# A two-block transformer kernel: the FFN's first gate projection taken one token block at a time, with half of its weights split ahead of the stage before

## The chip, the cores and the metric

The kernel runs on 1 core of one Trainium2 chip. The metric is the device time of one execution in microseconds; lower is better. Each version is run several times, and medians are compared.

## What is computed

The reference runs 256 tokens of width 2048 through a first block (two layers of several kinds of attention) and a second block of two layers. Only the second block is touched. Cut to what matters:

```python
for l in range(DEPTH):                      # DEPTH = 2
    u = rms_norm_2(h, norm_pre_mix[l])
    p = u @ w_in[l]                         # four recurrent mixers
    ...
    mixed = concatenate([o_ret, o_hgrn, o_ml, o_rw]) @ w_out[l]
    h = h + rms_norm_2(mixed, norm_post_mix[l])
    u = rms_norm_2(h, norm_pre_ffn[l])
    ffn = (silu(u @ w_ffn_gate[l]) * (u @ w_ffn_up[l])) @ w_ffn_down[l]
    h = h + rms_norm_2(ffn, norm_post_ffn[l])
```

The change sits at the two places, one in each layer, where the mixing stage ends and the FFN begins.

## The kernel before

The 256 tokens are two token blocks of 128 rows (`m` = 0, 1); the width of 2048 is 16 channel blocks of 128 (`kt`) in four groups (`g`). All products are float32 ones made of three float32r products: `weights` (line 211) loads 512 KB of a weight matrix into a tile `wraw`, ScalarE rounds it into `whi` (line 217), VectorE takes the rest into `wlo` (line 218), and `mm3` (line 223) issues hi x hi, hi x lo and lo x hi. One such load carries two channel blocks by 512 output columns; with both token blocks it feeds 12 matmuls of 512 columns. `wraw`, `whi` and `wlo` have three buffers each, so that a load waits until the split of the load three before it is done, and a split waits until TensorE is done with the weights three before. All loads are issued by SyncE's queue in a fixed order; a load that has to wait holds up all that stand behind it.

`mixing` (line 1639) ends with `out_group` (line 288) for the fourth mixer: eight loads of `w_out`, called O1 to O8 below. Then `old` (line 1675) fetches the eight tiles of the residual stream from DRAM (`keep`, 256 KB each). `last_group` (line 1585) takes the last mixer's eight loads of `w_out`, called L0 to L7 below: L0 to L3 as usual; L4 to L7 go into tiles of the tag `xt`, and these two column blocks are finished for token block 0 first, then for token block 1. VectorE adds each result to `acc` (line 1594), ScalarE squares it (line 1596), VectorE multiplies by a gain (lines 1598 and 1633). From the sums of squares a chain of small VectorE operations makes the reciprocal root (lines 1622, 1623 and 378 to 384), and `add_scaled` (line 1634) forms the new `X` from it.

`ffn` (line 1685) turns `X` on TensorE (line 317, into the two PSUM banks `t`), and `put` splits the turned tiles into `xt` on ScalarE (line 310) and VectorE (line 311). With `apart=2` the first two of the four groups are turned for token block 0 first and token block 1 after it, and the other two for both together. `by_tokens` (line 226) then goes through the 16 channel blocks, each with both token blocks, for 512 columns of the gate, then of the up projection; 11 such column blocks follow each other.

The order on each engine is made by a scheduler that moves instructions of the written program past each other, by its own estimate of when each can start; it is fixed before the run.

Of the kernel before, what the change touches and what calls it, by code (L numbers as in the profile page):

```python
# [11 lines left out]
FR = mybir.dt.float32r  # L12
# [6 lines left out]
P = 128  # L19
# [115 lines left out]
def halves(x):  # L135

    return [x[:, m] for m in range(2)]


class Emitter:  # L140
# [84 lines left out]
    def by_tokens(self, xg, w, c0, n):  # L225

        out = [self.bank("m") for _ in range(2)]
        j = min(16, 1 << int(math.log2(1024 // n)))
        for k in range(0, 16, j):
            wt = self.weights(w[k * P : (k + j) * P, c0 : c0 + n], j, n)  # L230
            for i in range(j):
                kt = k + i
                for m in range(2):
                    x = self.x_part(xg, kt, slice(m * P, m * P + P))
                    self.mm3(out[m][:, :n], x, [q[:, i] for q in wt], kt == 0, kt == 15)
            next(self.side, None)
        return [o[:, :n] for o in out]

    def by_channels(self, xg, w, c0, n):

# [1398 lines left out]
    def mixing(self, l, X):  # L1639
        nc = self.nc  # L1640
        w = self.a["w_in_2"][l]
        self.phase(**BANKS_MIX)
        keep = self.dp.tile([4, P, 2, 512], FT, name="keep")
        xg = self.x_pairs(X, self.c(f"premix{l}"))
        rows = self.row_scale_of(X)
        self.R = Later(lambda i: self.spread_rows(rows["r"]))

        def table(m):
            tb = self.t([P, 4, 64], "rtab")
            for i, (n, f) in enumerate((("cos64", 1.0), ("sin64", 1.0), ("cos64", 0.125), ("sin64", 0.125))):  # L1650
                nc.vector.tensor_scalar(tb[:, i], self.c(n)[:, m * 64 : m * 64 + 64], rows["r"][:, m : m + 1], f,
                                        OP.mult, OP.mult)
            return tb

        tabs = Later(table)
        ys = [self.pair("yt") for _ in range(4)]
        with self.using(x="r", small="esmall"):
            self.rwkv(l, X, keep, xg, w, ys[3])
        gates = self.mlstm_gates(l, xg, w, rows)
        for hf in range(2):  # L1660
            self.mlstm(l, hf, xg, w, rows, gates, ys[2])
        self.hgrn(l, 0, xg, w, ys[1])
        acc = [halves(self.t([P, 2, 512], "X")) for _ in range(4)]
        wo = self.a["w_out_2"][l]
        self.out_group(ys[2], wo, 2 * 512, acc, True)
        self.hgrn(l, 1, xg, w, ys[1])
        self.retention(0, xg, w, rows, tabs, ys[0])
        self.out_group(ys[1], wo, 512, acc, False)
        self.retention(1, xg, w, rows, tabs, ys[0])
        for _ in self.side:  # L1670
            pass
        self.out_group(ys[3], wo, 3 * 512, acc, False)

        def old(g, m):

            x = self.t([P, 512], "g2")
            nc.vector.tensor_copy(x[:, :1], acc[3][1][:, :1])
            nc.sync.dma_start(x, keep[g, :, m])
            return x

        olds = [[old(g, m) for m in range(2)] for g in range(4)]
        pg, r = self.last_group(ys[0], wo, 0, acc, self.a["norm_post_mix_2"][l])
        return self.add_scaled(acc, acc, pg, r, olds)

    def ffn(self, l, X):
        nc = self.nc
        self.phase(**BANKS_FFN)
        wg, wu, wd = (self.a[f"w_ffn_{n}_2"][l] for n in ("gate", "up", "down"))
        xg = self.x_pairs(X, self.c(f"preffn{l}"), apart=2)
        rows = self.row_scale_of(X)  # L1690
        acc = [[self.t([P, 512], "r2") for _ in range(2)] for _ in range(4)]
        last = None
        for g in range(11):
            ps = self.by_tokens(xg, wg, g * 512, 512)
            s = [self.t([P, 512], "g2") for _ in range(2)]
            for m in range(2):
                nc.scalar.activation(s[m], ps[m], AF.Silu, scale=rows["r"][:, m : m + 1])
            ps = self.by_tokens(xg, wu, g * 512, 512)
            for m in range(2):
                nc.vector.scalar_tensor_tensor(s[m], ps[m], rows["r"][:, m : m + 1], s[m], OP.mult, OP.mult)  # L1700
            if last is not None:
                self.out_group(last, wd, (g - 1) * 512, acc, g == 1)
            last = self.pair("yt")
            for m in range(2):
                self.y_turn(last, m, s[m])
        pg, r = self.last_group(last, wd, 10 * 512, acc, self.a["norm_post_ffn_2"][l])
        return self.add_scaled(X, acc, pg, r, X)
# [130 lines left out]
```

## Time and profile before

| what | us |
|---|---|
| median of 3 runs | 3941.05 |
| lowest and highest run | 3933.78, 3945.38 |
| the profiled execution's own time | 3934.05 |
| its span in the profile | 3932.2 |

The profile is of one execution. It gives for each engine its instructions in order of time, with the idle time before each and the instruction whose end released it; for SyncE's queue the issues of the loads; for the DMA engines the time from issue to landing. PE is TensorE, DVE is VectorE, ACT is ScalarE, SPq is SyncE's queue. Matmul starts are measured, their ends are modelled. The granted TensorE clock is given as a share of 2.4 GHz.

### The profile page before, as it was taken

To read this page: it belongs to the slowest core of one execution; us is meant where nothing else is said; L and a number is where in the kernel's file an instruction comes from. 1 tells how busy PE (TensorE), PEld (TensorE's weight loads), DVE (VectorE), ACT (ScalarE), POOL (GpSimd) and SP (SyncE) were. 2 spreads that over 40 slices of the span, in tenths; PEclk is the share of its full clock that TensorE was granted. 3 is DMA by queue.
4 is the path that set the end of the run, shared out by engine and by line. 5 is a ranking of instruction groups with operands and counts; after the bars stand their busy time and mean duration, and the time that the engine had idled before them with its cause. 6 is when DMAs were issued, how large, how long until landed. Compare 5 with 4: busy or idle time off the path is not lost.

```text
span 3932.2 us, 54691 instructions
## 1 busy us (share of the span) xinstructions
PE 3843.8 (98%) x21408; PEld 3220.0 (82%) x21408; DVE 2376.1 (60%) x4126; ACT 1806.8 (46%) x2455; POOL 0.2 (0%) x4
## 2 busy tenths in 40 slices
PE   9999999999999999999999999999999999999998
PEld 7878877788889988878888888888888878888886
DVE  6666677666665565664555556764666565555556
ACT  5545455554543554354443434543554354444433
POOL 0000000000000000000000000000000000000000
PEclk9999999999999999999999999998999999999999
DMA  7664544655643333566666666543334656666665
GB/s 237 193 175 129 165 142 144 177 161 166 198 120 108 108 107 116 170 188 187 186 183 187 183 187 192 152 119 97 92 113 123 188 172 187 183 187 185 186 185 166
DMA packets 402644, 633.64 MB, mean 161 GB/s; under 512 B 28081, under 2 KB 164017, under 8 KB 402385
## 3 DMA queue, kind: packets, MB, share of 16 engines
q1 hardware_dynamic: 399744, 624.70, 53.1%
q10 hardware_dynamic: 2640, 5.44, 0.4%
q8 instruction: 168, 2.75, 0.3%
q14 instruction: 92, 0.75, 0.1%
HBM read 623.77 MB, written 6.29 MB: 160 GB/s over the span
## 4 chain that ended last, share of the span: by engine, by line
PE 77%; DVE 5%; ACT 2%; DMA 2%; issue 1%; DVEq 0%; SPq 0%; ACTq 0%
PE b L223 66%; PE b L317 3%; DVE wlo L218 1%; PE b L1492 1%; PE b L1486 1%; ACT whi L217 1%; PE b L1188 1%; PE b L1092 1%; PE b L1178 1%; DMA g<-in_decay_dram 0%; PE b L1465 0%; PE b L471 0%; PE b L1268 0%; PE b L505 0%; DMA wraw<-in_w_ffn_down_dram 0%
## 5 line engine op out<-in xcount | busy, mean ns | idle before, releaser
L218 DVE TENSOR_TENSOR wlo<-wraw,whi 128x1024 fp32r<-128x1024 f32 x1144 | 1392.5, 1218 | 1080.7 <-ACT whi L217 1078.1
L217 ACT CAST whi<-wraw 128x1024 fp32r<-128x1024 f32 x1144 | 1195.9, 1046 | 1579.6 <-PE b L223 1462.2
L223 PE MATMUL b<-whi,xt 128*128 128x512 f32 (+1 forms) x5888 | 1694.3, 370 | 0.5 <-ACT g L1060 0.5
L223 PEld LDWEIGHTS b<-whi,xt 128*128 128x128 f32 x5888 | 1056.7, 189 | 194.2 <-issue 2.2
L223 PE MATMUL b<-wlo,xt 128*128 128x512 f32 (+1 forms) x2944 | 1083.2, 368 | 3.3 <-DVE wlo L218 3.1
L223 PE MATMUL b<-whi,yt 128*128 128x512 f32 x2304 | 745.1, 400 | 1.5 <-ACT yt L307 1.5
L223 PEld LDWEIGHTS b<-wlo,xt 128*128 128x128 f32 x2944 | 555.3, 189 | 101.9 <-DVE wlo L218 7.6
L223 PEld LDWEIGHTS b<-whi,yt 128*128 128x128 f32 x2304 | 432.6, 188 | 105.2 <-ACT yt L307 2.0
L223 PE MATMUL b<-xt,whi 128*128 128x256 f32 (+3 forms) x2688 | 516.5, 290 | 2.3 <-ACT xt L310 2.0
L223 PE MATMUL b<-wlo,yt 128*128 128x512 f32 x1152 | 459.0, 399 | 0.0
L223 PEld LDWEIGHTS b<-xt,whi 128*128 128x128 f32 (+3 forms) x2688 | 418.4, 189 | 19.2 <-issue 9.3
L223 PE MATMUL b<-xt,wlo 128*128 128x256 f32 (+3 forms) x1344 | 386.0, 287 | 0.0
L223 PEld LDWEIGHTS b<-wlo,yt 128*128 128x128 f32 x1152 | 217.2, 189 | 50.7 <-issue 0.6
L223 PEld LDWEIGHTS b<-xt,wlo 128*128 128x128 f32 (+3 forms) x1344 | 254.0, 189 | 3.9 <-issue 2.1
L223 PE MATMUL b<-whi,g 128*128 128x512 f32 (+1 forms) x384 | 108.1, 361 | 0.4 <-ACT g L307 0.4
L296 DVE TENSOR_TENSOR r<-b,r 128x512 f32<-128x512 f32 x144 | 92.2, 682 | 0.0
L223 PEld LDWEIGHTS b<-whi,g 128*128 128x128 f32 (+1 forms) x384 | 61.7, 162 | 14.3 <-ACT g L307 0.9
L317 PE MATMUL b<-gains,X 128*128 128x128 f32 x232 | 38.0, 300 | 32.6 <-DVE small L384 15.6
L223 PE MATMUL b<-wlo,g 128*128 128x512 f32 (+1 forms) x192 | 68.8, 358 | 0.0
L296 DVE TENSOR_TENSOR X<-b,X 128x512 f32<-128x512 f32 x96 | 62.7, 684 | 5.4 <-PE b L223 5.4
L317 PEld LDWEIGHTS b<-gains,X 128*128 128x128 f32 x232 | 29.9, 155 | 39.4 <-issue 26.0
L485 ACT ACTIVATE soft<-b,small,esmall 128x256 f32<-128x256 f32 (+1 forms) x88 | 44.9, 517 | 36.2 <-DVE small L482 32.6
(468 smaller groups left out, 2855.8 us busy)
## 6 DMA issues: line engine op xcount, KB each, us to landing
wraw<-in_w_in_dram SPq DMA_DIRECT2D x248, 512.0 KB, 3.7
wraw<-in_w_ffn_gate_dram SPq DMA_DIRECT2D x176, 512.0 KB, 3.7
wraw<-in_w_ffn_up_dram SPq DMA_DIRECT2D x176, 512.0 KB, 3.7
wraw<-in_w_ffn_down_dram SPq DMA_DIRECT2D x176, 512.0 KB, 3.7
wraw<-in_w_out_dram SPq DMA_DIRECT2D x128, 512.0 KB, 3.7
wraw<-in_even_w_in_dram SPq DMA_DIRECT2D x104, 512.0 KB, 3.6
wraw<-in_odd_w_in_dram SPq DMA_DIRECT2D x96, 512.0 KB, 3.7
wraw<-in_mem_w_kv_dram SPq DMA_DIRECT2D x32, 512.0 KB, 3.8
```

What stands on the lines that cost most here:

```text
L217: nc.scalar.copy(hi, raw)
L218: nc.vector.tensor_sub(lo, raw, hi.bitcast(FT))
L223: self.nc.tensor.matmul(out, l[x], r[y], start=start and i == 0, stop=stop and i == 2, **kw)
L296: self.nc.vector.tensor_add(dst[cb][m], ps[m], dst[cb][m])
L317: self.nc.tensor.transpose(o, s, self.c("ident")[:n, :n])
L485: nc.scalar.activation(pt[:, i], ps3[:, i], AF.Exp, scale=fs[:, i : i + 1], bias=nb[:, i : i + 1], accum_out=sm[:, i : i + 1])
L1092: self.nc.tensor.matmul(res[par][:, c], kT[r, i, ss], qT[r, i, ts], start=True, stop=True)
L1178: nc.tensor.matmul(pss[par][:, i], ek[r, i], eq[r, i], start=True, stop=True)
L1188: nc.tensor.matmul(out, vc[:, i * P + 64 * par : i * P + 64 * par + 64], am[:, par, i], start=False, stop=h == 1, skip_group_check=True)
L1486: mm(ps[:, i].rearrange("p (b k) -> p b k", k=h), gb[0][:, i], left(inv[:, i]), start=True, stop=True)
L1492: mm(ps[:, i], it[:, i], pl[:, i], start=True, stop=True)
```

## The change

A new function `ahead` loads the first eight channel blocks of the first 512 gate columns (four loads of 512 KB, called G0 to G3 below) and splits them into 16 tiles of the tag `r2`, which the mixers have left by then. It is written before `last_group`. A new function `by_tokens_after` takes the place of `by_tokens` for the first gate block: it uses these eight, loads three more pairs, runs 14 channel blocks with token block 0, then the same 14 with token block 1, and then the last two with both. `apart` is 4, so that all four groups of `X` are turned for token block 0 before token block 1. The arithmetic and the bytes loaded are the same.

```diff
+    def ahead(self, w, c0):
+        nc = self.nc
+        res = []
+        for k in range(0, 8, 2):
+            raw = self.t([P, 1024], "wraw").rearrange("p (j c) -> p j c", j=2)
+            nc.sync.dma_start(raw, w[k * P : (k + 2) * P, c0 : c0 + 512].rearrange("(j p) c -> p j c", p=P))
+            for i in range(2):
+                pair = [self.t([P, 512], "r2", FR) for _ in range(2)]
+                self.split(pair, raw[:, i])
+                res.append(pair)
+        return res
+
+    def by_tokens_after(self, xg, w, c0, first):
+        out = [self.bank("m") for _ in range(2)]
+        wts = list(first)
+        for k in range(8, 14, 2):
+            wt = self.weights(w[k * P : (k + 2) * P, c0 : c0 + 512], 2, 512)
+            wts += [[q[:, i] for q in wt] for i in range(2)]
+        for m in range(2):
+            for kt in range(14):
+                self.mm3(out[m], self.x_part(xg, kt, slice(m * P, m * P + P)), wts[kt], kt == 0, False)
+        wt = self.weights(w[14 * P :, c0 : c0 + 512], 2, 512)
+        for m in range(2):
+            for i in range(2):
+                self.mm3(out[m], self.x_part(xg, 14 + i, slice(m * P, m * P + P)), [q[:, i] for q in wt], False, i == 1)
+        return out
...
         olds = [[old(g, m) for m in range(2)] for g in range(4)]
+        self.first = self.ahead(self.a["w_ffn_gate_2"][l], 0)
         pg, r = self.last_group(ys[0], wo, 0, acc, self.a["norm_post_mix_2"][l])
...
-        xg = self.x_pairs(X, self.c(f"preffn{l}"), apart=2)
+        xg = self.x_pairs(X, self.c(f"preffn{l}"), apart=4)
...
-            ps = self.by_tokens(xg, wg, g * 512, 512)
+            ps = self.by_tokens(xg, wg, g * 512, 512) if g else self.by_tokens_after(xg, wg, 0, self.first)
```

The new lines shift the old ones: a line between 238 and 1681 has 29 added to it in the changed kernel (so 311 is 340 there and 1594 is 1623), and one behind that 30.

**SyncE's queue, end of the first layer's mixing.** Before, the `w_out` loads here are L0, then L1 to L4, then (behind the residual tiles) L5 to L7:

```order
L1602 DMA y<-in_norm_post_mix_dram 128x512
L216 DMA wraw<-in_w_out_dram 128x2x512
L1602 DMA y<-in_norm_post_mix_dram 128x512
L216 DMA wraw<-in_w_out_dram 128x2x512 x4
L1678 DMA g_15721<-keep 128x512
...
L1678 DMA g_15742<-keep 128x512
L216 DMA wraw<-in_w_out_dram 128x2x512 x3
L1602 DMA y<-in_norm_post_mix_dram 128x512
L216 DMA wraw<-in_w_ffn_gate_dram 128x2x512
```

Now:

```order
L1631 DMA y<-in_norm_post_mix_dram 128x512
L245 DMA wraw<-in_w_ffn_gate_dram 128x2x512
L1631 DMA y<-in_norm_post_mix_dram 128x512
L245 DMA wraw<-in_w_ffn_gate_dram 128x2x512 x3
L216 DMA wraw<-in_w_out_dram 128x2x512 x2
L1707 DMA g_15721<-keep 128x512
...
L1707 DMA g_15742<-keep 128x512
L216 DMA wraw<-in_w_out_dram 128x2x512 x3
L1631 DMA y<-in_norm_post_mix_dram 128x512
L216 DMA wraw<-in_w_out_dram 128x2x512 x3
L216 DMA wraw<-in_w_ffn_gate_dram 128x2x512 x2
```

G0 to G3 stand where L0 to L3 stood; L0 and L1 follow them, and L2 to L7 stand behind the eight residual tiles, where before only L5 to L7 did.

**VectorE, the same place.** Before, behind the adds of `out_group` (X<-b) stand the splits of L0 and L1, then the copies of one column that go before the residual fetches, then the splits of L2 and L3:

```order
L296 TENSOR_TENSOR X<-b_15642,X 128x512
L218 TENSOR_TENSOR wlo<-wraw,whi 128x1024 x2
L296 TENSOR_TENSOR X<-b_15681,X 128x512
L296 TENSOR_TENSOR X<-b_15682,X 128x512
L1677 COPY g_15721<-X 128x1
...
L1677 COPY g_15742<-X 128x1
L218 TENSOR_TENSOR wlo<-wraw,whi 128x1024 x2
```

Now:

```order
L325 TENSOR_TENSOR X<-b_15642,X 128x512
L337 TENSOR_TENSOR r_15748<-wraw,r_15747 128x512
...
L337 TENSOR_TENSOR r_15772<-wraw,r_15771 128x512
L325 TENSOR_TENSOR X<-b_15681,X 128x512
L325 TENSOR_TENSOR X<-b_15682,X 128x512
L337 TENSOR_TENSOR r_15778<-wraw,r_15777 128x512
L1706 COPY g_15721<-X 128x1
...
L1706 COPY g_15742<-X 128x1
L337 TENSOR_TENSOR r_15782<-wraw,r_15781 128x512
L218 TENSOR_TENSOR wlo<-wraw,whi 128x1024 x2
```

Six splits of G0 to G2 and the first of G3 now stand ahead of the eight copies, and the second of G3 ahead of the splits of L0 and L1.

**VectorE, around the last result of `last_group`** (b_15938 before, b_15978 now: token block 1, last column block). Before:

```order
L1622 TENSOR_REDUCE small<-ss 128x1
L1594 TENSOR_TENSOR X<-b_15938,X 128x512
L1623 TENSOR_SCALAR small<-small 128x1
L1598 TENSOR_TENSOR X<-X,y 128x512
L378 TENSOR_SCALAR small<-small 128x1
L218 TENSOR_TENSOR wlo<-wraw,whi 128x1024
L379 TENSOR_SCALAR small<-small 128x1
L380 TENSOR_SCALAR small<-small 128x1
L1633 TENSOR_TENSOR X<-X,y 128x512
```

Now:

```order
L1651 TENSOR_REDUCE small<-ss 128x1
L218 TENSOR_TENSOR wlo<-wraw,whi 128x1024
L1652 TENSOR_SCALAR small<-small 128x1
L1627 TENSOR_TENSOR X<-X,y 128x512
L407 TENSOR_SCALAR small<-small 128x1
L1623 TENSOR_TENSOR X<-b_15978,X 128x512
L408 TENSOR_SCALAR small<-small 128x1
L409 TENSOR_SCALAR small<-small 128x1
L1662 TENSOR_TENSOR X<-X,y 128x512
```

The split of a gate load and one gain product, which stood behind the last result's add, now stand ahead of it. In both orders token block 0's root still stands behind the add of token block 1's last result.

## Rows read from the trace of the kernel before

**Rows 1.** The page, part 1: busy us (share of the span) and instructions.

```profile
PE 3843.8 (98%) x21408; PEld 3220.0 (82%) x21408; DVE 2376.1 (60%) x4126; ACT 1806.8 (46%) x2455; POOL 0.2 (0%) x4
```

**Rows 2.** Waits of PE, 1640 to 1740 us: waiting <- releaser: total us, times, longest.

```profile
PE b L317 <- DVE small L384: 7.8, 1, 7.8
PE b L223 <- ACT xt L217: 1.5, 1, 1.5
```

**Rows 3.** The same waits in the second layer, 3105 to 3205 us.

```profile
PE b L223 <- ACT xt L217: 0.8, 1, 0.8
```

**Rows 4.** PE timeline, 1670 to 1740 us: start, us, instructions, [idle before <- releaser].

```profile
1683.70 0.63 PE L223 MATMUL b<-whi,yt 128*128 128x512 f32 x2
...
1684.40 0.40 PE L223 MATMUL b<-whi,yt 128*128 128x512 f32 x1
1684.63 1.55 PE L223 MATMUL b<-xt,yt 128*128 128x512 f32 x6
1687.64 10.02 PE L223 MATMUL b<-xt,yt 128*128 128x512 f32 x42 [1.46 <-ACT xt L217]
1705.44 1.94 PE L317 MATMUL b<-gains,X 128*128 128x128 f32 x8 [7.78 <-DVE small L384]
1707.03 0.78 PE L223 MATMUL b<-whi,xt 128*128 128x512 f32 x1
...
1711.37 0.40 PE L223 MATMUL b<-wlo,xt 128*128 128x512 f32 x1
```

**Rows 5.** SyncE's queue, timeline 1630 to 1740 us: start, us, what was issued.

```profile
1661.62 0.37 SPq L216 DMA_DIRECT2D wraw<-in_w_out_dram  x1
...
1665.15 8.39 SPq L216 DMA_DIRECT2D wraw<-in_w_out_dram  x4
1674.56 4.07 SPq L1678 DMA_DIRECT2D g<-keep  x8
1679.05 2.42 SPq L216 DMA_DIRECT2D wraw<-in_w_out_dram  x3
...
1688.87 0.37 SPq L216 DMA_DIRECT2D wraw<-in_w_ffn_gate_dram  x1
```

**Rows 6.** DMA issues, 1664 to 1666 and 1679 to 1680: KB each, us to landing.

```profile
wraw<-in_w_out_dram SPq DMA_DIRECT2D x1, 512.0 KB, 4.1
...
wraw<-in_w_out_dram SPq DMA_DIRECT2D x2, 512.0 KB, 7.8
```

**Rows 7.** DVE timeline, 1628 to 1740 us, around the residual copies.

```profile
1666.32 1.23 DVE L218 TENSOR_TENSOR wlo<-wraw,whi 128x1024 fp32r<-128x1024 f32 x1 [0.59 <-ACT whi L217]
1667.46 1.28 DVE L296 TENSOR_TENSOR X<-b,X 128x512 f32<-128x512 f32 x2
...
1674.38 0.58 DVE L1677 COPY g<-X 128x1 f32<-128x1 f32 x8
```

**Rows 8.** ACT timeline, 1670 to 1740 us: the splits of L4 and L5.

```profile
1677.39 1.04 ACT L217 CAST xt<-wraw 128x1024 fp32r<-128x1024 f32 x1
...
1686.54 1.04 ACT L217 CAST xt<-wraw 128x1024 fp32r<-128x1024 f32 x1 [5.82 <-DMA wraw<-in_w_out_dram]
```

**Rows 9.** Windows of 2 us: busy of PE, PEld, DVE, ACT, POOL, PE clock, DMA share, GB/s.

```profile
1682.00:1684.00 2.00, 2.00 (x10) 1.59 (x10) 0.28 (x1) 0.00 (x0) 0.00 (x0) 1.00 1.05 399
...
1700.00:1702.00 2.00, 0.00 (x0) 0.00 (x0) 2.00 (x6) 0.31 (x2) 0.00 (x0) 0.75 0.78 251
...
1710.00:1712.00 2.00, 2.00 (x10) 1.54 (x9) 2.00 (x5) 2.00 (x8) 0.00 (x0) 0.69 0.00 0
```

**Rows 10.** DVE timeline, 1697 to 1705 us: between the last matmul and the turning of X.

```profile
1697.55 1.23 DVE L218 TENSOR_TENSOR wlo<-wraw,whi 128x1024 fp32r<-128x1024 f32 x1 [0.85 <-ACT whi L217]
...
1700.40 1.21 DVE L218 TENSOR_TENSOR wlo<-wraw,whi 128x1024 fp32r<-128x1024 f32 x1
...
1702.99 0.15 DVE L383 TENSOR_TENSOR small<-small 128x1 f32<-128x1 f32 x1
...
1704.54 0.75 DVE L1634 SCALAR_TENSOR_TENSOR X<-X,small,g 128x512 f32<-128x512 f32 x1
```

## The prediction

> **What bounds the kernel now.** I read the page first. TensorE is busy for 98% of the span [rows 1], so a change can only win where it stands still, and loses wherever it makes it stand still. Then I asked for TensorE's waits around the place that the change touches. In the first layer there are two that matter: 7.8 us until the reciprocal root of the mixing stage is there, and 1.5 us for the split of a `w_out` load [rows 2]; in the second layer the root's wait is the same 7.8 us and the other one 0.8 [rows 3]. I worked out the first layer and take the second as its copy.
>
> The timeline of TensorE shows what lies around them [rows 4]. Matmuls of 512 columns start 0.70 us apart for three, so a load's 12 take 2.8 us. The 7.78 us of idle time end with the turning of X, and from the first gate matmul on, at 1707.03, the rows follow each other without a gap. This is the first thing to see: behind the root's wait TensorE waits for nothing, so weights that are ready earlier have no wait there to take away.
>
> The second thing is what came before. L5's split began only when its load had landed; ScalarE had stood 5.82 us for it [rows 8]. The queue shows why: L5 to L7 were issued at 1679.05, behind eight residual tiles from 1674.56 on [rows 5], and took 7.8 us to land, where the one of 1665.15 had taken 4.1 [rows 6]. In 1682 to 1684 the DMA engines were full, at 399 GB/s [rows 9]. So the end of the mixing stage is where transfers are already late, and the change puts 2.1 MB more (G0 to G3) into the same queue ahead of the loads that TensorE waits for.
>
> **The change part by part, first layer.** Matmuls, bytes and turnings are the same in number; what changes is when. Before, O8's matmuls end at 1684.63 less four blocks of 2.8, that is 1673.4, and L0 follows at once.
>
> *L0, late.* G0 takes L0's place in the queue, at 1661.62, and G1 that of L1, at 1665.15 [rows 5]. G2 needs the buffer of O8, whose split ends at 1667.6 [rows 7]. G3 needs that of G0, whose two splits on VectorE stand behind the pair of adds that ends at 1668.7 [rows 7]; at 0.64 each (half of that pair's 1.28) they end at 1670.0. L0 needs the buffer of G1: landed at 1665.15 + 4.1 [rows 6] = 1669.25, rounded in 1.04 [rows 8], its last VectorE split done at about 1671.1. L0 is issued there and lands 4.1 later, at 1675.2. ScalarE is through with G3 by then (1670.0 + 4.1 + 1.04), so `whi` is there at 1676.2. VectorE has more ahead of it: the adds of O8 to 1675.1, a split of G3, the eight copies (0.58, [rows 7]) and G3's other split, to 1676.9; then L0's own 1.23 [rows 7], to 1678.1. TensorE stands from 1673.4 to 1676.2, does the two matmuls that need `whi` alone, stands again, and ends L0 ten matmuls after 1678.1, at 1680.4 instead of 1676.2: **+4.2**.
>
> *L1.* It needs G2's buffer (landed 1672.0, split 1673.9) and lands at 1678.0; its split ends with L0's matmuls. No further wait; L1 ends at 1683.2.
>
> *L2, behind the residual tiles.* These wait for the copies, which now stand behind G3's first split, and go out from 1675.9 to 1680.0 (4.07 for eight, [rows 5]). L2 goes out at 1680.0 and lands as L5 did, 7.8 later [rows 6], at 1687.8; `whi` at 1688.9, `wlo` at 1690.1. TensorE waits from 1683.2, does two matmuls, and ends L2 at 1692.4 instead of 1686.0: **+6.4**. L3 to L7 come soon enough behind it, by the same steps. The old wait of L5, 1.46 [rows 4], is gone into this one: **-1.5**, in the second layer -0.8.
>
> *The clock.* After the 7.78 us wait the granted clock was 0.50 to 0.69 (1.2 GHz, half) until 1710 to 1712, and 1.00 (2.4 GHz) before it fell in 1700 to 1702 [rows 9]; the ten matmuls from 1707.03 to 1711.37 took 4.34 us [rows 4] instead of 2.33. After the 1.46 us wait nothing slowed. L2's wait of 5.7 us is nearer to the first: **+2.0**. L0's, 2.8 us, is nearer to the second: 0, at most 2.0. The Trainium skill's page "TensorE: Matmul & The Clock Gate", section "HAM oscillation", says that a matmul group which follows a wait for a transfer starts throttled again, group after group; by that L0's wait would cost the 2.0 too, and the sum be 4 us higher.
>
> *The root's wait, shorter.* Before, two VectorE splits of gate loads lay in it, at 1697.55 and 1700.40 [rows 10]. In the new order both are ahead of the last add. What is left behind the last matmul: that add (0.64), two small ones, a gain product (0.64), three small ones, a gain product, then 15 small ones; 16 of those took 1.55 from 1702.99 to 1704.54 [rows 10], so 0.1 each. With 0.75 for the first new X and 0.2 to the turning that is about 4.6 instead of 7.78: **-3.2**. Bounds: 0, if a gate load lands so late that its split still lies in the wait, and -3.2 as counted.
>
> *The gate's first block.* With weights there, the splits of X decide. ScalarE and VectorE have 16 pieces for token block 0 to make, with eight squarings between them, while TensorE runs 42 matmuls, 10 to 12 us; before, they had the same number of pieces for as many matmuls, plus splits of weights, and TensorE ran without a gap [rows 4]. The turnings now wait for PSUM banks in the middle of the pass: 0 to 1.3, taken as **+0.6**. The last two channel blocks need a buffer that token block 1's tenth frees; it is 2.8 us ahead of need, and so is the up projection's first load.
>
> Sum of a layer: 4.2 + 6.4 - 1.5 + 2.0 - 3.2 + 0.6 = 8.5; second layer 9.2. Together **+17.7**. On the profiled execution's 3934.05 that is 3951.8; that execution lies 7 below the median of the runs, 3941.05, on which it is **3958.7**. Lower bound: L0 waits for `whi` alone (2.8), L2 lands in 4.1 in spite of what is ahead of it (ready at 1686.4, +2.7), the clock holds, the gate's block gains nothing and loses nothing: 0.8 and 1.5, together +2. Upper: both waits slow the clock, no gain at the root, 1.3 in the gate: 14.4 and 15.1, together +30.
>
> **The rivals.** (1) *The loads are hidden.* L0 used to be issued 11.8 us before its use and needs some 6.4 of them, so there are 5.4 us of slack for four loads. Then only the shorter root counts, and the old waits may go too: -1.5 - 0.8 - 2 x 3.2 = -8.7, 3932.4, no change that can be told. Against it: L5 was late without the extra loads. The Trainium skill's "Trainium Kernel Development and Optimization", section "Best Practices", asks for double buffering, so that transfers lie under compute; by that rule this is what the change should give. Its rows here, L5's 7.8 us to landing and the full engines, speak against the rule.
>
> (2) *Only the bytes count.* Order and buffers adapt, and the stage is longer by 2.1 MB at the 399 GB/s of its full windows [rows 9], 5.3 us a layer, less 3.2: +4.1 in all, 3945.2, no change that can be told. The Trainium skill's "DMA: Bandwidth & Descriptors", section "Bandwidth", puts a core's share of HBM at about 358 GB/s; by it this would be +5.3. The 399 of the row is above that, and the row is used.
>
> (3) *Faster: the clock holds.* If the loads are hidden as in (1) and the root's wait, 4.6 us instead of 7.78, is short enough that the clock does not fall, the ten slow matmuls (2.0) and eight slow turnings (1.94 instead of about 1.0, [rows 4]) go as well: -8.7 - 2 x 2.9 = -14.5, 3926.6. The point lies somewhere between 1.46 and 7.78 us of standing still; nothing says it is above 4.6, and L2's wait speaks against it.
>
> **How the numbers follow.** About 0.3%, 12 us, is what a measurement of this kernel can tell from none. The forecast has 0.68; by its bounds (+2 to +30) about 0.07 of that stays under 12. Rival (1) has 0.14, (2) 0.12, (3) 0.06. So slower 0.61, same 0.33, faster 0.06. The range leaves out (3) and most of (1): 3935 to 3972. The forecast's own, with the runs' spread of 6 either way, is 3943 to 3972.
>
> **What would show it.** Right: in the changed trace TensorE's waits before the turning of X are one of 3 to 4 us at L0 and one of 5 to 7 at L2, both on ScalarE's or VectorE's split and behind it on a `w_out` load; L2's issue stands behind the eight residual tiles near 1680; the root's wait is 4 to 5.5; half clock follows L2's wait. Wrong: L0 and L2 start on time, or the root's wait stays at 7.8, or gaps of more than 2 us appear within the gate's first block. If the time is lower by over 12 us, the reading that transfers bound this stage is wrong as a whole.

## The result, and the profile after

| | before | changed |
|---|---|---|
| median of 5 runs each, us | 3941.05 | 3958.42 |
| lowest and highest | 3933.78, 3945.38 | 3955.01, 3967.46 |
| span of the profiled execution | 3932.2 | 3956.6 |
| mean granted clock of it | 0.983 | 0.978 |

The changed kernel is slower: ratio 1.0053, 95% interval 1.0039 to 1.0068. The forecast was 3958.7, slower.

The page's first part, to be set beside [rows 1], shows the same number of matmuls and 24 instructions more on VectorE and on ScalarE each. The work did not grow; it stands elsewhere.

```profile
PE 3862.7 (98%) x21408; PEld 3233.6 (82%) x21408; DVE 2381.5 (60%) x4150; ACT 1813.9 (46%) x2479; POOL 0.2 (0%) x4
```

TensorE's waits from 1640 to 1760 us answer to [rows 2]; columns are total us, times, longest.

```profile
PE b L223 <- ACT whi L217: 6.3, 2, 3.8
PE b L346 <- DVE small L412: 6.0, 1, 6.0
...
PE b L223 <- DVE wlo L218: 0.5, 1, 0.5
PE b L223 <- ACT xt L339: 0.4, 2, 0.3
```

The second layer, 3110 to 3225 us, answers to [rows 3]:

```profile
PE b L223 <- ACT whi L217: 6.9, 2, 4.4
PE b L346 <- DVE small L412: 6.5, 1, 6.5
```

The wait for the root is shorter, the old wait of L5 is gone, and two new waits for ScalarE's `whi` have come, with as many microseconds as the root's. SyncE's queue, against [rows 5], tells which loads they are:

```profile
1667.46 0.37 SPq L245 DMA_DIRECT2D wraw<-in_w_ffn_gate_dram  x1
...
1670.99 5.16 SPq L245 DMA_DIRECT2D wraw<-in_w_ffn_gate_dram  x3
1677.12 2.20 SPq L216 DMA_DIRECT2D wraw<-in_w_out_dram  x2
1680.82 4.15 SPq L1707 DMA_DIRECT2D g<-keep  x8
1685.06 2.33 SPq L216 DMA_DIRECT2D wraw<-in_w_out_dram  x3
```

G0 takes the place that L0 had, 5.84 us later than there because of what happened upstream (below). L0 goes out at 1677.12; L2 at 1685.06, right behind the eight residual tiles. TensorE's timeline, against [rows 4], has the waits that answer:

```profile
1683.24 1.22 PE L223 MATMUL b<-whi,yt 128*128 128x512 f32 x2 [3.83 <-ACT whi L217]
...
1694.47 0.73 PE L223 MATMUL b<-whi,yt 128*128 128x512 f32 x2 [2.47 <-ACT whi L217]
1695.73 0.59 PE L223 MATMUL b<-wlo,yt 128*128 128x512 f32 x1 [0.52 <-DVE wlo L218]
...
1702.50 11.05 PE L223 MATMUL b<-xt,yt 128*128 128x512 f32 x48
1719.55 1.94 PE L346 MATMUL b<-gains,X 128*128 128x128 f32 x8 [6.00 <-DVE small L412]
```

The first is L0, the second L2, the last the turning of X; L3 to L7 come without a wait. Two matmuls that took 0.63 us in [rows 4] take 1.22 at L0. The windows around them (columns as in [rows 9]) say why, by the column in front of the DMA share:

```profile
1674.00:1682.00 8.00, 5.40 (x24) 4.01 (x22) 7.23 (x19) 3.42 (x6) 0.00 (x0) 1.00 0.82 265
1682.00:1690.00 8.00, 6.72 (x17) 4.85 (x18) 2.45 (x2) 2.09 (x2) 0.00 (x0) 0.57 0.91 297
1690.00:1694.00 4.00, 2.00 (x9) 1.30 (x7) 2.56 (x4) 1.93 (x5) 0.00 (x0) 1.00 0.92 348
1694.00:1698.00 4.00, 3.00 (x8) 2.11 (x9) 3.71 (x4) 2.31 (x3) 0.00 (x0) 0.75 0.53 152
```

The granted clock fell to half (1.2 GHz) twice in these windows, once at each wait. A mean of 0.57 over 8 us is half clock for 6.9 of them, at L0; L2's spell begins at 1696.0 and lasts 3.4 us, 2.0 of them in the last window.

VectorE between the last matmul (1713.55) and the turning, against [rows 10]:

```profile
1711.48 1.22 DVE L218 TENSOR_TENSOR wlo<-wraw,whi 128x1024 fp32r<-128x1024 f32 x1
...
1713.16 1.23 DVE L218 TENSOR_TENSOR wlo<-wraw,whi 128x1024 fp32r<-128x1024 f32 x1 [0.40 <-ACT whi L217]
...
1715.03 0.68 DVE L1623 TENSOR_TENSOR X<-b,X 128x512 f32<-128x512 f32 x1
...
1718.65 0.75 DVE L1663 SCALAR_TENSOR_TENSOR X<-X,small,g 128x512 f32<-128x512 f32 x1
```

Of the two gate splits that stood in the root's wait before, one is now ahead of the last matmul and the other still behind it: its load had landed late, and the wait of 0.40 us in front of it ended with ScalarE's rounding.

**Where the 24.4 us of the two spans lie.** From the first changed place on the queue (G0's issue, L0's before) to the first product of the up projection, the change costs 8.34 us in the first layer (1667.46 to 1770.34, against 1661.62 to 1756.16) and 9.53 in the second. That is 17.9. Upstream of it, where both kernels have the same order, 5.84 are lost, and 0.7 lie elsewhere. The 5.84 are mostly one spell of half clock of 10.2 us that begins at 1651.6 and loses half of them, 5.1. The profiled execution of before has such a spell at this place in the second layer only; ten of the twelve profiles below have it in both, two of them of kernels that differ from the one before only behind this place. So it belongs to the execution, and the change's own cost is the 17.9, close to the 17.4 between the medians.

The three stretches of the second layer, where both executions have such a spell (6.8 us in the changed kernel, 10.2 before, so that 1.7 us less are lost): from the last `w_in` matmul to the last `w_out` matmul, the root's wait with the first turning, and the first gate and up blocks. Before:

```profile
3097.20:3155.70 58.50, 56.26 (x239) 44.25 (x237) 37.25 (x69) 21.80 (x31) 0.00 (x0) 0.91 0.64 205
3155.70:3165.10 9.40, 1.59 (x9) 1.58 (x9) 9.17 (x37) 3.81 (x10) 0.00 (x0) 0.65 0.58 187
3165.10:3214.20 49.10, 49.10 (x217) 38.84 (x216) 31.16 (x63) 28.55 (x54) 0.00 (x0) 0.96 0.51 147
```

Changed:

```profile
3114.40:3181.80 67.40, 58.74 (x239) 45.53 (x237) 44.06 (x78) 27.96 (x42) 0.00 (x0) 0.87 0.65 211
3181.80:3189.90 8.10, 1.62 (x9) 1.65 (x9) 7.95 (x34) 2.49 (x8) 0.00 (x0) 0.65 0.62 195
3189.90:3239.10 49.20, 48.58 (x217) 38.10 (x216) 28.23 (x69) 27.39 (x58) 0.00 (x0) 0.99 0.34 106
```

The mixing stage is 8.9 us longer (10.6 with the clock of before), the root's wait 1.3 shorter, the gate's block as long as it was. The experiments are read by these three stretches, called *mixing*, *root* and *gate* below.

### The profile page after: what moved, and what is told of

It reads as the page before. It is cut to its first block, busy times and chain, and to the rows that moved or that the text cites. A ratio compares the mean times of both kernels' runs of the same rounds, so it can differ in the third digit from the quotient of the medians.

```text
span 3956.6 us, 54721 instructions
## 1 busy us (share of the span) xinstructions
PE 3862.7 (98%) x21408; PEld 3233.6 (82%) x21408; DVE 2381.5 (60%) x4150; ACT 1813.9 (46%) x2479; POOL 0.2 (0%) x4
## 3 DMA queue, kind: packets, MB, share of 16 engines
q1 hardware_dynamic: 399744, 624.70, 49.7%
## 4 chain that ended last, share of the span: by engine, by line
PE 77%; DVE 5%; ACT 3%; DMA 2%; issue 1%; SPq 0%; DVEq 0%; ACTq 0%
PE b L223 66%; PE b L346 3%; DVE wlo L218 1%; ACT whi L217 1%; PE b L1521 1%; PE b L1515 1%; PE b L1217 1%; DMA wraw<-in_w_out_dram 1%; PE b L1121 1%; PE b L1207 1%; PE b L1494 1%; PE b L500 0%; PE b L1297 0%; DMA wraw<-in_w_ffn_gate_dram 0%; PE b L534 0%
## 5 line engine op out<-in xcount | busy, mean ns | idle before, releaser
L223 PE MATMUL b<-whi,xt 128*128 128x512 f32 (+1 forms) x5824 | 1669.8, 369 | 0.7 <-ACT g L1089 0.5
L223 PEld LDWEIGHTS b<-whi,xt 128*128 128x128 f32 x5824 | 1043.4, 188 | 190.5 <-issue 2.2
L223 PE MATMUL b<-wlo,xt 128*128 128x512 f32 (+1 forms) x2912 | 1069.5, 367 | 3.0 <-DVE wlo L218 2.8
L223 PE MATMUL b<-whi,yt 128*128 128x512 f32 x2304 | 753.3, 403 | 14.7 <-ACT whi L217 13.2
L325 DVE TENSOR_TENSOR X<-b,X 128x512 f32<-128x512 f32 x96 | 62.8, 684 | 6.5 <-PE b L223 6.4
L339 ACT ACTIVATE xt<-b,gains 128x128 fp32r<-128x128 f32 (+1 forms) x128 | 50.5, 420 | 20.9 <-DVE xt L340 12.7
```

Of the source, the lines that this page charges most:

```text
L223: self.nc.tensor.matmul(out, l[x], r[y], start=start and i == 0, stop=stop and i == 2, **kw)
L325: self.nc.vector.tensor_add(dst[cb][m], ps[m], dst[cb][m])
L339: nc.scalar.activation(hi, src, AF.Identity, scale=scale)
```

## The experiments

Each was timed beside the kernel before on the same chip; the medians of before were 3940.4, 3939.0 and 3939.4 in the three groups of four, from 29 to 35 runs.

### Is it the place in the queue? `late`

```diff
-        self.first = self.ahead(self.a["w_ffn_gate_2"][l], 0)
         pg, r = self.last_group(ys[0], wo, 0, acc, self.a["norm_post_mix_2"][l])
+        self.first = self.ahead(self.a["w_ffn_gate_2"][l], 0)
```

> The change, but its four gate loads G0 to G3 are issued behind L7 instead of ahead of L0; the FFN's order (14 blocks with one token block alone, then the other) stays as changed. Theory (queue): the loss of 17.4 us is made by G0 to G3 standing ahead of L0 in the queue and in the three raw buffers. Then the waits at L0 and L2 go, L5's old wait of about 1.5 us is back, the root's wait is 7 to 9 us again (gate splits stand in it as before), and the time is that of before within 8 us: 3933 to 3949. Rival (FFN): the loss lies in the one-token-block order and the turning of X; then it stays, 3953 to 3963, with no new wait in front of the root. Rival (bytes): the stage is short of transfer time whatever the order; G0 to G3 behind L7 then delay the gate's own loads, with a new gap of 3 us or more in the gate's first block.

Measured: 3951.2, ratio 1.0032 (1.0019 to 1.0045). The waits at L0 and L2 are gone, L5's is back (1.7 us, 1.0 in the second layer), and the mixing is 58.7 us in both layers, as before. That part of the theory holds. The time does not (3933 to 3949 was expected), because the root's wait is 11.1 us in both layers. VectorE in it (six splits of G's halves, line 337, and two of the loads behind them):

```profile
1708.35 0.68 DVE L337 TENSOR_TENSOR r<-wraw,r 128x512 fp32r<-128x512 f32 x1
...
1714.95 0.69 DVE L337 TENSOR_TENSOR r<-wraw,r 128x512 fp32r<-128x512 f32 x1
...
1715.70 1.22 DVE L218 TENSOR_TENSOR wlo<-wraw,whi 128x1024 fp32r<-128x1024 f32 x1
...
1717.02 1.23 DVE L218 TENSOR_TENSOR wlo<-wraw,whi 128x1024 fp32r<-128x1024 f32 x1
```

Eight splits where before had two [rows 10]. More tiles that can be split ahead means more splits that come before the root.

### The turning alone: `apart4`

```diff
-        xg = self.x_pairs(X, self.c(f"preffn{l}"), apart=2)
+        xg = self.x_pairs(X, self.c(f"preffn{l}"), apart=4)
```

> The kernel before, with only the turning of X changed: all four groups for token block 0 first, then token block 1; the gate goes through the channel blocks with both token blocks as before. Theory (queue): nothing in front of the root moves; the gate's first channel blocks need token block 1 early, so up to 3 us a layer could be lost in the gate's first block, none of it in front of the root: 3938 to 3947, same as before. Rival (FFN): a good part of the 17.4 us is here, 3949 or more.

Measured: 3949.9, ratio 1.0025 (1.0016 to 1.0035): the rival's number, not the theory's. The mixing is as before; the gate's stretch is 53.0 us in the first layer and 54.2 in the second, where it was 49.1. TensorE is idle in it for 3.4 of the 53.0:

```profile
1712.60:1765.60 53.00, 49.64 (x217) 38.02 (x216) 32.66 (x71) 30.52 (x62) 0.00 (x0) 0.99 0.46 139
```

The longest of these waits, 1.8 us at 1721.55, is that of a turning, for VectorE's split of an earlier turned tile. As I read it, with both token blocks in each channel block, token block 1 is asked for before it is turned. The changed kernel asks for it 14 blocks later and has 49.2 us in the same stretch, so this cost is not in its 17.4: turning order and pass order belong together, and the one without the other is dear.

### Half the dose: `half`

```diff
     def ahead(self, w, c0):
...
-        for k in range(0, 8, 2):
+        for k in range(0, 4, 2):
...
     def by_tokens_after(self, xg, w, c0, first):
...
-        for k in range(8, 14, 2):
+        for k in range(4, 10, 2):
...
-            for kt in range(14):
+            for kt in range(10):
...
+        for k in range(10, 16, 2):
...
```

The last three pairs of blocks go with both token blocks.

> The change with half the dose: two gate loads (G0, G1, four channel blocks) ahead of L0, ten channel blocks in the one-token-block pass, six with both. In the queue L0 to L4 now stand ahead of the residual tiles and L5 to L7 behind them, as before the change. Theory (queue): L0 takes the buffer of O8's split and is issued near 1667.6 instead of about 1671, so TensorE waits for it 0 to 1.5 us and the clock does not fall; L2 no longer stands behind the residual tiles, and its wait of 2.5 us goes; L5 waits 1 to 3 us as before; the root's wait is 6 to 7.8 us. Sum 0 to +3 a layer: 3939 to 3949, not half of the loss but less. Rival (bytes): half of the bytes, half of the loss, 3950. Rival (FFN): the order of the passes sets it, 3953 or more.

Measured: 3943.9, ratio 1.0011 (1.0000 to 1.0022), as the theory had it. No wait is over 1 us in the mixing, the clock does not fall at L0, the root's wait is 6.8 us in both layers; the mixing is 60.7 and 60.8 us, still 2.2 longer than before at the same clock. A fifth of the loss for half of the bytes, with ten blocks still taken one token block at a time: neither the bytes nor the order of the passes sets it alone.

### Further ahead in the queue: `early`

```diff
+        self.first = self.ahead(self.a["w_ffn_gate_2"][l], 0)
         self.out_group(ys[3], wo, 3 * 512, acc, False)
...
-        self.first = self.ahead(self.a["w_ffn_gate_2"][l], 0)
```

> The change with all four gate loads moved further ahead in the queue, in front of O1 (the first of the eight loads of the projection before), where the raw buffers come free sooner than the loads are needed; L0 to L4 then stand ahead of the residual tiles, as in the kernel before. Same bytes before the root as in the change. Theory (queue): L0 and L2 are on time, L5's wait of 1 to 1.5 us is back, the gate splits are out of the root's wait, which is 4.5 to 6.5 us: 0 to -3 us a layer, so 3932 to 3945. Rival (bytes): 2.1 MB more before the root cost the same wherever they stand, 3953 or more. Rival (FFN): also 3953 or more, but then with no new wait before the root. If O1 to O3 come late for these loads, a wait of 2 us or more shows in front of them, which is the queue theory again at another place.

Measured: 3949.8, ratio 1.0026 (1.0016 to 1.0037), above the theory's range. The clause on O1 came true: 

```profile
1644.20 0.74 PE L223 MATMUL b<-whi,yt 128*128 128x512 f32 x2 [1.71 <-ACT whi L217]
1645.46 0.80 PE L223 MATMUL b<-wlo,yt 128*128 128x512 f32 x1 [0.52 <-DVE wlo L218]
```

The half clock that follows lasts 17.1 us in both layers instead of 10.2, a loss of 3.4 us a layer. And the root's wait is 7.7 and 8.0: nothing won. VectorE's timeline has splits of gate loads that begin at 1705.05 and 1707.90, where the last matmul ends at 1705.2. They are those of the next loads. As I read it, the raw buffers and the `wlo` tiles come free when TensorE is through with L3, and whatever gate load is next in the program is split there.

### Outside the three buffers: `apart_from_ring`

```diff
-            raw = self.t([P, 1024], "wraw").rearrange("p (j c) -> p j c", j=2)
+            raw = self.t([P, 512], "g2")
...
+        self.first = self.ahead(self.a["w_ffn_gate_2"][l], 0)
         self.out_group(ys[3], wo, 3 * 512, acc, False)
```

> The change with the gate's eight blocks loaded ahead as eight loads of 256 KB into tiles of the tag g2 instead of the three raw buffers, and called ahead of the projection before; in the queue they stand together between its loads' first five and the rest, L0 to L5 ahead of the residual tiles and L6, L7 behind. Same bytes, same split tiles, same order in the FFN. Theory (queue and ring): nothing holds L0 or L2 back, so the last matmul of the mixing stage is as early as before (58.6 us from the last w_in matmul, with 10.2 us of half clock, as in the second layer before), L5's old wait may go too; the root's wait is 7 to 8 us, since the raw buffers are free for the gate's next loads and their splits come there as in the run with the gate loads further ahead. 3937 to 3946. Rival (bytes): 2.1 MB more before the root cost 5 us a layer wherever they stand, 3950 or more. Rival (FFN order): 3950 or more, with the loss behind the first gate matmul.

Measured: 3945.2, ratio 1.0013 (1.0001 to 1.0025). All eight blocks ahead, the same bytes, a third of the loss. The root's wait is 6.8 and 7.0, near the 7 to 8 expected. The mixing is longer than expected: 62.8 us (with 13.7 of half clock) and 60.3 (with 10.2), where 58.6 was expected. That is 1.7 us more than before in the second layer, at the same clock, and not the 5 of the rival that counts bytes, which falls by this and by the time.

### The second wait alone: `residual_behind`

```diff
             nc.vector.tensor_copy(x[:, :1], acc[3][1][:, :1])
-            nc.sync.dma_start(x, keep[g, :, m])
             return x
...
         pg, r = self.last_group(ys[0], wo, 0, acc, self.a["norm_post_mix_2"][l])
+        for g in range(4):
+            for m in range(2):
+                nc.sync.dma_start(olds[g][m], keep[g, :, m])
```

> The change, but the eight residual tiles are issued among and behind the loads of the last projection: two of them ahead of L2 instead of eight, the others between L4 and the end. G0 to G3 still ahead of L0. Theory (queue): L0 is as late as in the changed kernel, 3.8 to 4.4 us, with a spell of half clock behind it; L2's wait (2.5 + 0.5 us) and the spell behind it (3.4 us of half clock, 1.7 us lost) go; about 4 us a layer less than the change: 3948 to 3954. Rival: L2 is late because of L0 and the three buffers, and the residual tiles ahead of it cost nothing: then its wait stays and the time is 3955 to 3962.

Measured: 3951.7, ratio 1.0031 (1.0019 to 1.0043), 6.7 below the changed kernel; that one was timed in another group, and the two intervals overlap. The traces are closer: from G0's issue to the up projection's first product there are 99.6 and 99.4 us, in the changed kernel 102.9 and 103.3. TensorE's waits over 0.5 us from L0 on, first layer:

```profile
1679.77 1.22 PE L223 MATMUL b<-whi,yt 128*128 128x512 f32 x2 [3.69 <-ACT whi L217]
1697.56 9.04 PE L223 MATMUL b<-xt,yt 128*128 128x512 f32 x36 [0.56 <-ACT xt L217]
1713.51 1.73 PE L346 MATMUL b<-gains,X 128*128 128x128 f32 x7 [6.91 <-DVE small L411]
```

L0 is as late as in the changed kernel, with half clock behind it for the same 6.8 us; L2's wait and its spell are gone. So the eight residual tiles make L2 late, as the theory says, and that is worth 3.3 and 4.0 us a layer by the traces. Against the kernel before (94.5 and 93.8 us) 5.0 and 5.6 are left, and L0's wait and spell account for them.

### The splits out of the root's wait: `splits_behind_root`

```diff
         nc.scalar.copy(hi, raw)
+        if behind is not None:
+            nc.vector.tensor_copy(lo[:, 0, :1], behind)
         nc.vector.tensor_sub(lo, raw, hi.bitcast(FT))
```

`behind` is a column of the new X of token block 1, and it is given for the three loads that follow G3.

> The change, with the VectorE splits of the gate's next three loads held back by a copy of one column that needs the new X of token block 1; queue and loads as in the change. Theory: the two splits of 1.22 us that stood in the root's wait leave it, so the wait falls from 6.0 and 6.5 us to 3.6 to 4.2; the first gate block has TensorE work of eight channel blocks before it needs the held splits, so at least half of this is kept: 3951 to 3957. Rival: the splits are missing in the gate's first block instead, where VectorE is then late: the wait falls, gaps of 2 us appear behind the first gate matmuls, and the time stays 3957 to 3962.

Measured: 3958.2, ratio 1.0039 (1.0026 to 1.0052) to before, the same as the changed kernel. The rival holds, with gaps shorter than its 2 us. The root's wait fell to 3.0 and 2.8 us, further than expected, and the gate's stretch grew from 49.2 to 52.4 and 51.0. Its waits in the first layer, all on VectorE:

```profile
PE b L225 <- DVE xt L342: 1.7, 2, 1.3
PE b L225 <- DVE wlo L220: 0.3, 1, 0.3
```

The second layer has the same waits. In the first the clock falls once more behind the longest of them, for 3.4 us:

```profile
1728.35 1.09 PE L225 MATMUL b<-whi,xt 128*128 128x512 f32 x2 [1.34 <-DVE xt L342]
```

```profile
1726.00:1728.00 2.00, 1.00 (x4) 0.49 (x3) 2.00 (x3) 1.21 (x4) 0.00 (x0) 1.00 0.52 102
1730.00:1732.00 2.00, 2.00 (x8) 1.62 (x7) 0.98 (x6) 0.37 (x1) 0.00 (x0) 0.50 0.89 321
```

From G0's issue to the up projection's first product the first layer gains nothing (103.0 us, 102.9 in the changed kernel); the second, where the clock holds in the gate's stretch, gains 2.4 in this trace (101.0 against 103.3). The medians show no gain.

The same on the kernel before (`before_splits_behind_root`, second and third gate load):

> The kernel before, with the VectorE splits of the gate's second and third load held back by a copy of one column that needs the new X of token block 1 (nothing loaded ahead, turning and order as before). Theory: two splits leave the root's wait, which falls from 7.8 to 5.2 to 6.6 us; the gate's first load feeds 12 matmuls, 4 to 5 us at half clock, and the second's split is about ready then: 3932 to 3939. Rival: the gate needs them at once with both token blocks, so the gain comes back as a wait in the first gate block: 3939 to 3945 with gaps of 1 to 3 us there. If so, loading weights ahead is what makes room to hold them back.

Measured: 3948.9, ratio 1.0023 (1.0012 to 1.0035), slower than either expectation. The root's wait fell from 7.8 to 4.6 and 6.2, and the gate's stretch went from 49.1 to 54.1 and 53.2, with one wait of 2.8 and 3.1 us for `wlo`. VectorE is nearly full from the last matmul on (16.0 of the 16.4 us behind it); a split of 1.2 us that is moved within this stretch comes back.

### The residual tiles in the kernel before: `before_residual_behind`

The edit of `residual_behind`, on the kernel before.

> The kernel before, with the residual tiles issued among and behind L5 to L7 instead of all eight ahead of L5. Theory (queue): L5 is issued about 3 us earlier and lands sooner, so its wait of 1.5 us (second layer 0.8) goes and nothing else changes; the root still finds its tiles: 3935 to 3940, no half clock lost or won. Rival: L5's wait only moves to L6 or L7, or the last residual tiles now come late to the root: 3939 to 3944.

Measured: 3938.4, ratio 1.0002 (0.9993 to 1.0011). No change that can be told. L5's wait is gone as the theory says, but the root's wait is 8.9 and 9.7 us. VectorE stands 1.05 us for a row of gains and 0.99 for the rounding of a gate load, which the queue both brings later now, and two whole gate splits stand behind the last matmul (1700.7):

```profile
1700.67 0.69 DVE L1633 TENSOR_TENSOR X<-X,y 128x512 f32<-128x512 f32 x1 [1.05 <-DMA y<-in_norm_post_mix_dram]
...
1703.07 1.22 DVE L218 TENSOR_TENSOR wlo<-wraw,whi 128x1024 fp32r<-128x1024 f32 x1 [0.99 <-ACT whi L217]
...
1705.67 1.22 DVE L218 TENSOR_TENSOR wlo<-wraw,whi 128x1024 fp32r<-128x1024 f32 x1
```

That is the rival's second half in kind, though it is a row of gains and a gate load that come late there, not the residual tiles: what is moved ahead of one wait is missing at the next.

The same on `half` (`half_residual_behind`):

> The run with half of the blocks ahead (3943.9), with the residual tiles moved among and behind L5 to L7. Theory (queue): its waits of 1.0 us for L5 and about 1 us behind it go, the root's wait stays 6.8 us: 3939 to 3943, still not faster than before, since three splits of 1.22 us stand between the last matmuls and the root. Rival: the residual tiles are not what its mixing stage loses (60.7 us from the last w_in matmul against 58.6 at the same clock before): 3942 to 3946.

Measured: 3941.2, ratio 1.0008 (0.9999 to 1.0017), in the theory's range and 0.8 below the rival's, which is less than can be told. L5's wait is gone, a wait of 1.0 and 0.8 us for VectorE's add of an earlier result is still there, and the root's wait grew here too, to 7.5 and 7.3.

### Another engine for the splits: `before_splits_on_gpsimd`, `half_splits_on_gpsimd`

```diff
-        nc.vector.tensor_sub(lo, raw, hi.bitcast(FT))
+        (lo_on or nc.vector).tensor_sub(lo, raw, hi.bitcast(FT))
```

`lo_on` is GpSimd for the second and third gate load of the kernel before, and for the three loads behind the preloaded ones in `half_residual_behind`.

> The kernel before, with the splits (wlo) of the gate's second and third load made by GpSimd, which is idle, instead of VectorE; nothing else moved. Theory: the root's wait is 7.8 us because two VectorE splits of 1.2 us stand in it, and holding them back only moved them into the first gate block because VectorE is full there too. On GpSimd they leave both: the wait falls to 4.6 to 6.2 us and the first gate block is as long as before (49 us): 3933 to 3938. Rival: GpSimd needs more than about 5 us for such a split, or slows VectorE beside it, and TensorE waits for wlo in the first gate block: 3940 to 3950.

> The run with half of the blocks ahead and the residual tiles behind, with the splits of the next three gate loads made by GpSimd. Theory: the three VectorE splits leave the root's wait, which falls from 6.8 to 3.0 to 4.5 us, and the four blocks that are ready give GpSimd the time of 24 matmuls, 6 us or more, for its first one: 3931 to 3938, the first of these kernels below the one before. Rival: as in the run before this one, GpSimd is too slow or disturbs VectorE: 3940 to 3950, with a wait for wlo in the first gate block.

Measured: 3943.2, ratio 1.0009 (0.9998 to 1.0019), and 3947.2, ratio 1.0019 (1.0009 to 1.0029). Both rivals by their times, but not by their wait: TensorE waits for `wlo` in the gate's first block for no more than 0.4 us. A split takes GpSimd 2.55 us. But the root's wait in the first is 8.6 us, with no split of VectorE's in it. GpSimd's timeline and VectorE's beside it:

```profile
1701.26 5.10 POOL L218 TENSOR_TENSOR wlo<-wraw,whi 128x1024 fp32r<-128x1024 f32 x2 [1700.82 <-ACT whi L217]
```

```profile
1701.92 2.24 DVE L1633 TENSOR_TENSOR X<-X,y 128x512 f32<-128x512 f32 x1
...
1704.58 0.68 DVE L1594 TENSOR_TENSOR X<-b,X 128x512 f32<-128x512 f32 x1
1705.18 1.20 DVE L382 TENSOR_TENSOR small<-small 128x1 f32<-128x1 f32 x1
1706.30 0.68 DVE L1598 TENSOR_TENSOR X<-X,y 128x512 f32<-128x512 f32 x1
```

The gain product, 0.68 us elsewhere (as the one at 1706.30), lasted 2.24, until just after GpSimd's first split (1701.26 + 2.55 = 1703.81); a product of single columns, 0.15 elsewhere, lasted 1.20, until the end of the second (1706.36). The add from PSUM between them took its usual 0.68.

In the second, the root's wait did fall, from 7.5 and 7.3 us to 5.0 and 5.1, but the gate's stretch grew from 49.4 and 49.7 to 54.6 and 54.3. VectorE's products that make the new X, 0.74 us elsewhere, run there beside GpSimd's splits:

```profile
1709.72 2.78 DVE L1665 SCALAR_TENSOR_TENSOR X<-X,small,g 128x512 f32<-128x512 f32 x1
...
1713.03 2.24 DVE L1665 SCALAR_TENSOR_TENSOR X<-X,small,g 128x512 f32<-128x512 f32 x1
```

None of the twelve is faster than the kernel before by more than can be told.

## Why the prediction was right

**What bounds the stage** was read rightly: nothing behind the root waits for weights, and what is loaded ahead takes the place of loads that are waited for. `late`, which leaves L0 its place, and `half` and `apart_from_ring`, which issue it early enough, have no wait of more than 0.4 us for it.

**The sum, part by part.** The last matmul of the mixing stage against before, shifted by the 5.84 (and 15.29) of the issue; then the root's wait; then the gate's stretch:

| us | forecast | first layer | second layer |
|---|---|---|---|
| mixing (L0, L2, clock, old L5) | +11.1, second +11.8 | +10.1 | +10.8 |
| root's wait | -3.2 | -1.8 | -1.3 |
| gate's first block | +0.6 | +0.1 | +0.1 |
| together | +8.5, +9.2 | +8.3 | +9.5 |

Of the signs that the text had named, L0's wait (3 to 4 us), L2's place in the queue and the half clock behind L2 came as said, the second layer's L0 a little above; L2's wait (5 to 7) and the root's (4 to 5.5) did not.

*L0's issue* was forecast at 1671.1, which with the 5.84 is 1676.9; it was 1677.1. ScalarE began on it 5.0 us later instead of 4.1, which made TensorE's first stand 3.8 us long and not 2.8. L2's was forecast at 1685.8 and was 1685.1, behind the residual tiles, and it landed 7.5 us later (forecast 7.8).

*The step that failed* is the clock's: "L0's, 2.8 us, is nearer to the second: 0, at most 2.0". The wait was 3.8 and 4.4 us, and the clock was half for 6.8 us, from shortly before the wait's end. The 24 matmuls of L0 and L1 took 8.6 us (1683.24 to 1691.84) instead of 5.6; at most 0.4 of the difference is a wait for `wlo`, so the clock cost 2.6, more than the upper bound. The Trainium skill's page "TensorE: Matmul & The Clock Gate", section "HAM oscillation", which says that a group behind a wait for a transfer starts throttled again, was right here: the trace has 1.22 us for two matmuls at L0 that take 0.63 otherwise. L5's wait of 1.46 us before, for a transfer too, had left the clock at full [rows 4, 9].

*Why the sum held all the same*: two terms erred by as much, in opposite directions. L0 and L1 ended 7.0 us later than before, where 4.2 was forecast; L2 with its slow clock added 5.1, where 6.4 + 2.0 was; and 2.0 came back behind it, where 1.5 was; together 10.1 in the first layer. L2's waits were forecast at 5.7 and then 0.8 us and were 2.5 and 0.5. L0's and L1's slow matmuls ran while L2 was under way. L2's landing set the end, not TensorE, so the slow clock used up the wait that was forecast for L2 (L0 and L1 ended 2.8 us later than forecast, and L2 had 3.5 less waiting). The text had not seen this: that its clock term did the sum no harm is luck. Where L2 is in time, in `residual_behind`, nothing takes up the slow clock: L0 and L1 take 8.7 and 8.8 us there instead of 5.6, and with L0's wait of 3.7 and 3.9 that is 6.8 and 7.1 a layer; the root's wait is 0.9 and 1.7 shorter, and the kernel is 12.7 us over before, 6.4 a layer. So the Trainium skill's rule was right about the clock at L0, and the 4 us more that it would have made of the sum did not come, for this reason.

*The root's wait* was mis-sized: -3.2 forecast, -1.8 and -1.3 measured. The terms that the text lists for what is left (three operations of 0.64, 20 small ones of 0.1, then 0.75 and 0.2) add up to 4.9 and not 4.6, so that -2.9 would have been its number. The rest is the bound that the text named, a gate load that lands late: one split of 1.23 us is still in the wait. `early` shows the reason more plainly: with all of G split long before, two gate splits still stand there. The buffers refill, so loading ahead does not clear that wait.

*The gate's block*: 0.4 to 0.5 us of waits, as forecast; the clock came back a little sooner behind the shorter root's wait and paid for them. The bounds of 0 and 1.3 held.

**The rivals.** The first (loads hidden) falls with the two waits. The second (bytes) asked for 3945.2, 13 less than measured, and falls with the mixing of `apart_from_ring`. The third (the clock holds behind a short wait for the root) falls too: in `splits_behind_root` that wait is 2.8 to 3.0 us, and there is still a spell of half clock behind it, of 3.4 us. The point "between 1.46 and 7.78 us" of which that rival spoke is not there (last section).

**What stays open.** Nothing was run that leaves L0 its place, has L2 and L5 in time and also keeps VectorE's stretch at the root as short as in `splits_behind_root`; the runs say only that each of these was paid for by another. Of the 17.4 us, some part is the spells upstream, which differ between executions: one minus the mean granted clock, times the span, averages 85.5 us over the five runs of the changed kernel and 75.8 over 29 of the one before, 9.7 more, where the two sites in the profile account for about 7 (two times 5.1 in the mixing, less 1.7 each behind the root, where the spell is 6.8 us and was 10.2). The rest was not traced.

## What to carry to other kernels

A load that is issued ahead is cheap only if it makes no load late that is needed sooner, in the queue or in the buffers, and if its splits do not land in a wait for the engine that makes them (`late`); before loading ahead, look up what stands behind it in the same queue and which three splits free its buffers. Where a wait ends on a chain of a full engine, moving that engine's other work out of the wait pays only if there is idle time of this engine to move it to: here no run that took splits out of the root's wait was faster by the medians, because the stretch behind it grew. And a wait in front of one load can hide the cost of a wait ahead of it, so a forecast should add up ends, not waits.

## What the runs showed of the hardware

The length of a wait did not decide whether the clock fell. It fell to half for 3.4 us behind L2's waits of 2.47 and 0.52 us in the changed kernel, behind one of 1.97 us in `before_splits_behind_root` and behind one of 1.34 us in the first layer of `splits_behind_root`. Waits of 1.46 us (before [rows 4, 9]), 1.69 (`late`) and 1.79 (`apart4`) left it at full in the first layer, and so did the same 1.34 us in the second layer of `splits_behind_root`; what else decided is open.

VectorE's operations on two tiles of SBUF did not end before a GpSimd split that ran beside them did: 2.24 us instead of 0.68, and 1.20 instead of 0.15 for one column, while an add that reads PSUM took its 0.68 (`before_splits_on_gpsimd`). The Trainium skill's page "SBUF — State Buffer", section "SBUF: two separate sides", states this as an exclusive lock on a port pair that the two engines share, held for the whole instruction; the trace agrees. From these rows, an estimate: a split handed to GpSimd can hold up VectorE for up to 2.55 us, more than the 1.22 that VectorE needs for it.
